# The first block of attention scores in three passes of split operands

## The chip, the cores and the metric

The kernel runs on one core of one Trainium2 chip. The metric is the device time of one execution in microseconds (us). The profile shows five engines of the core: TensorE for matrix products, with its weight loads shown apart, VectorE and ScalarE for element-wise work, GpSimd and SyncE, which here mostly issue transfers.

## What is computed

A decoder trunk of two layers over 256 tokens with width 1024, batch 1, all in float32. Layer 0 mixes tokens with a "forgetting" attention (a bias from cumulated log forget gates), layer 1 with a block-sparse attention whose block of 256 is here the whole sequence, so that it is causal attention with a relative-position bias. Each layer goes on with a SwiGLU feed-forward of width 2816 and a gated input embedding; a norm ends it. Both attentions have 16 heads of 64 and compute, for each head:

```python
logits = jnp.einsum('bhqd,bhkd->bhqk', qblk, k).astype(jnp.float32) * scale
logits = logits + cq[..., None] - c[:, :, None, :]          # layer 1: + table_ht[:, _t5_bucket(rel_o)]
logits = jnp.where(key_pos[None, :] <= t[:, None], logits, -jnp.inf)
probs = jax.nn.softmax(logits, axis=-1).astype(v.dtype)
return jnp.einsum('bhqk,bhkd->bhqd', probs, v)
```

Queries 0 to 127 see keys 0 to 127 alone; queries 128 to 255 see all 256.

## The kernel before

Most matmuls work on split operands. A float32 value x is kept as a high half, hi (x rounded to the type `float32r`), and a low half, lo = x - hi, and a product is three passes: hi·hi, hi·lo and lo·hi, each a matmul of `float32r`. `mm3` (lines 92 to 96) does so for the projections and the feed-forward. Weights arrive by DMA as float32; ScalarE copies them to the high half (line 169, 187 or 139) and VectorE subtracts for the low half (171, 188 or 142). TensorE loads the stationary operand of each matmul by an instruction of its own, which the profile shows as PEld.

An attention layer works on pairs of heads, j = 0 to 7; the two heads of a pair lie in partitions 0 to 63 and 64 to 127. For each pair `project(j, 0)` and `project(j, 1)` compute q and k, 24 matmuls of 128x128 by 256 columns each, into one bank `pq`. Then `project` scales the bank by the norm's rows into `t` ("qkt", line 563: q for 256 tokens, then k for 256), and makes the halves `th` ("qkh", 569, ScalarE) and `tl` ("qkl", 571, VectorE). These halves leave out the first 128 columns of `t`, the queries 0 to 127, so they hold 384 columns: q of the later 128 tokens and k of all 256.

`scores(*js)` (581) takes two pairs, four heads, at a time: after pairs 2, 4 and 6 for the two pairs before the last one projected, and once for pairs 6 and 7, with a part of the product for v between. So each layer has four calls. In a call each head has a bank `sp` with 384 columns: columns 0 to 127 are the first block (queries 0 to 127 against keys 0 to 127), columns 128 to 383 the other queries against all keys. In layer 0 four matmuls (405) first add the forget-gate bias to all 384 columns. Then the first block follows as a float32 matmul for each head, straight from `t` (589), and the other columns in three passes over the split halves (592), pass by pass, and the four heads in turn in each pass. In some calls the product of earlier pairs with v (674 and 676, float32) follows. VectorE then adds the mask or bias and takes minima (606), ScalarE exponentiates (610), and the results are transposed (644), sent through DMA to their place (651, 659) and read by `values`.

Each engine runs its instructions in the order in which they stand in its queue; the code places some by hand with `tc.issue_after`.

Of the kernel before, what the change touches and what calls it, by code (L numbers as in the profile page):

```python
# [28 lines left out]
F32R = mybir.dt.float32r  # L29
# [3 lines left out]
P = 128  # L33
S = 256
# [41 lines left out]
def trunk(ctx: ExitStack, tc: tile.TileContext, xg, wx, xr, pt, w, cst, gf, rel, hot, rvm, out):  # L76
    nc = tc.nc
    one = ctx.enter_context(tc.tile_pool(name="one", bufs=1))
    work = ctx.enter_context(tc.tile_pool(name="work", bufs=2))
# [4 lines left out]
    def bank(name):  # L84
        return ps.tile([P, 512], F32, tag="bank", name=name)

    def f32(ap):
        return ap.bitcast(F32)

    mm = nc.tensor.matmul  # L90

    def mm3(o, a, b, start, stop):
        (ah, al), (bh, bl) = a, b
        mm(o, ah, bh, start=start, stop=False, skip_group_check=True)  # L94
        mm(o, ah, bl, start=False, stop=False, skip_group_check=True)  # L95
        return mm(o, al, bh, start=False, stop=stop, skip_group_check=True)  # L96
# [353 lines left out]
    def enter(bks, x, w, k):  # L450

        steps = [(hf, a, 0, t) for hf in range(2) for a in range(2) for t in range(2)]
        if k == 0:
            steps[1:3] = steps[2:0:-1]
        for hf, a, b, t in steps + [(hf, 0, 1, t) for hf in range(2) for t in range(2)]:
            got = mm(bks[2 * t + hf], x[a][:, t * P:(t + 1) * P], w[b][:, hf * HC:(hf + 1) * HC],  # L456
                     start=k + a + b == 0, stop=k + b == KT, skip_group_check=True)
        return got

    def attention(layer, nm, mid, early, nf):  # L460
# [4 lines left out]
        def row(k, hf, w):  # L465
            for t in range(2):
                got = tokens(vb[2 * t + hf], nm.k(k), t, w, k == 0, k == KT - 1)
            return got

        def cut(wt, a):  # L470
            return [w[:, a * HC:(a + 1) * HC] for w in wt]

        for c in range(4):
            wt = [early.pop(0) if early else half() for _ in range(2 if c < 2 else 1)]
            for kk in range(2):
                k = 2 * c + kk
                if c > 1:
                    got = row(k, 0, cut(wt[0], kk))
                elif layer == 0:
                    got = enter(vb, nm.k(k), wt[kk], k)  # L480
                else:
                    for hf in range(2):
                        got = row(k, hf, cut(wt[kk], hf))
                if layer == 0 and k == KT - 2:
# [4 lines left out]
                    bias, add = rest()  # L489
# [25 lines left out]
        def second(c, wt):  # L515
            for kk in range(2):
                got = row(2 * c + kk, 1, cut(wt, kk))
            return got
# [20 lines left out]
        def weights(j, a):  # L539
            with held(j - 2), held("t" if j in BEHIND and a else None):  # L540
                if j in BEHIND and a == 0:
                    return gapped()
                return blocks(ENTRY if layer and j + a == 0 else ())

        def project(j, a):
            hi, lo = ahead.pop(0) if ahead else weights(j, a)
            if a == 0:
                pq[j] = bank(f"pq{layer}_{j}")
            bk = pq[j]
            for k in range(KT):  # L550
                mm3(bk[:, a * S:(a + 1) * S], (hi[k], lo[k]), nm.k(k),
                    start=(k == 0), stop=(k == KT - 1))
            if a == 0:
                return
            del pq[j]
            far = fresh[:]
            fresh.clear()
            if far:
                ahead.extend(weights(j + 1, i) for i in range(2 if j + 1 < NP else 0))
            for x in far[:1]:  # L560
                scaled(*x)
            t = work.tile([P, 2, S], F32, tag="qkt", bufs=3, name=f"qkt{layer}_{j}")
            got = nc.vector.tensor_tensor(t.rearrange("p a s -> p (a s)"), bk,
                                          nm.row.rearrange("p a s -> p (a s)"), op=ALU.mult)
            marks["t"] = marks.get(j - 1, (got,))[0], got
            th = work.tile([P, 3 * P], F32R, tag="qkh", bufs=3, name=f"qkh{layer}_{j}")
            tl = work.tile([P, 3 * P], F32R, tag="qkl", bufs=3, name=f"qkl{layer}_{j}")
            src = t.rearrange("p a s -> p (a s)")[:, P:]
            first = nc.scalar.activation(th, src, AF.Copy)
            with tc.issue_after(got.ins):  # L570
                got = nc.vector.tensor_tensor(tl, src, f32(th), op=ALU.subtract)
            marks[j] = first, got
            qk[j] = t, th, tl
            for x in far[1:]:
                with tc.issue_after(first.ins):
                    scaled(*x)
            with tc.issue_after(got.ins):
                for back in [turn(*x[:2]) for x in far]:
                    back()

        def scores(*js, then=None):

            rows = [slice(s * DH, (s + 1) * DH) for s in range(2)]
            heads = [(2 * j + s, d, qk[j], bank(f"sp{layer}_{2 * j + s}")) for j in js for s, d in enumerate(rows)]
            if add:
                for i, _, _, sp in heads:
                    add(i, sp)
            for _, d, (t, _, _), sp in heads:
                mm(sp[:, 0:P], t[d, 0, 0:P], t[d, 1, 0:P], start=add is None, stop=True, skip_group_check=True)
            for n, (q, k) in enumerate(((1, 1), (1, 2), (2, 1))):  # L590
                for _, d, t, sp in heads:
                    got = mm(sp[:, P:3 * P], t[q][d, 0:P], t[k][d, P:], start=False, stop=n == 2,
                             skip_group_check=True)
            if then is not None:
                with tc.issue_after(got.ins):
                    got = values(then)
            sl = (slice(0, P), slice(P, 3 * P))
            for n, j in enumerate(js):
                del qk[j]
                e = work.tile([P, 2, 3 * P], F32, tag="e", bufs=4, name=f"e{layer}_{j}")  # L600

                mn = tiny.tile([P, 2, 2, 2], F32, tag="mn", bufs=4, name=f"mn{layer}_{j}")
                for s in range(2):
                    i, _, _, sp = heads[2 * n + s]
                    for q, b in enumerate(bias(i)):
                        marks["low"] = nc.vector.tensor_tensor_reduce(e[:, s, sl[q]], sp[:, sl[q]], b, 1.0, 3.0e38,
                                                                      ALU.add, ALU.min, mn[:, 0, s, q:q + 1])
                for s in range(2):
                    for q in range(2):
                        last = nc.scalar.activation(e[:, s, sl[q]], e[:, s, sl[q]], AF.Exp, scale=-1.0,  # L610
                                                    bias=mn[:, 0, s, q:q + 1], accum_out=mn[:, 1, s, q:q + 1])
                marks["e", j] = last,
                fresh.append((j, e, mn))
            return got
# [9 lines left out]
        def scaled(j, e, mn):  # L624

            rc = inverse(j, mn)
            for s in range(2):
                for q, c in enumerate((slice(0, P), slice(P, 3 * P))):
                    nc.scalar.activation(e[:, s, c], e[:, s, c], AF.Copy, scale=rc[:, s, q:q + 1])
            return rc  # L630
# [36 lines left out]
        def values(j):  # L667

            po = bank(f"po{layer}_{j}")
            heads = [(slice(s * DH, (s + 1) * DH), slice((2 * i + s) * DH, (2 * i + s + 1) * DH), pts.pop(2 * i + s),  # L670
                      po[:, (i - j) * S:(i - j + 1) * S]) for i in (j, j + 1) for s in range(2)]
            for n in (0, 2):
                for d, c, t, o in heads[n:n + 2]:
                    mm(o[d], v[:, 0, c], t[:, 0:2], start=True, stop=False, skip_group_check=True)
                for d, c, t, o in heads[n:n + 2]:
                    got = mm(o[d, P:S], v[:, 1, c], t[:, 2], start=False, stop=True, skip_group_check=True)
            marks["o"] = split(oh[:, j:j + 2], ol[:, j:j + 2], po.rearrange("p (j s) -> p j s", s=S))
            return got

        for j in range(NP):  # L680
            project(j, 0)
            if layer and j == 0:
# [5 lines left out]
                bias, add = mid(nm)()  # L688
# [3 lines left out]
            if j + 1 in BEHIND:  # L692
                got = scores(j - 2, j - 1, then=0 if j == 6 else None)
# [26 lines left out]
        def split_late(after):  # L720
            with held(after):
                return half()

        got = second(2, split_late(6))
# [3 lines left out]
        with tc.issue_after(got.ins):  # L728
            got = scores(NP - 2, NP - 1, then=2)
# [8 lines left out]
        with tc.issue_after(got.ins):  # L738
            got = second(3, wt)
        keep(1)  # L740
        got = behind(got, "mid", 0)
        got = behind(got, "low", 1, 2)
        with tc.issue_after(got.ins):
            got = values(4)
        marks["third"] = marks["o"]
        got = behind(got, "seven", 3, 4)
        with tc.issue_after(got.ins):
            got = values(6)
# [245 lines left out]
    for layer in range(2):  # L994
# [5 lines left out]
        got = []  # L1000
# [127 lines left out]
```

## Time and profile before

| | us |
|---|---|
| median of 3 runs | 634.96 |
| lowest and highest run | 634.74, 635.93 |
| the profiled execution | 634.63 |
| its span, from the first to the last instruction | 632.8 |

The profile is one execution seen by the hardware profiler. Times of a line are in us, means of one instruction in ns. TensorE's matmuls are pipelined: a matmul's duration in the rows is the time from its start to its end, while the next one starts long before that end, so the time that it costs is read from the chain, or from starts. An operand of type `float32r` stands as f32 in the rows of matmuls. A float32 matmul appears as two records. TensorE's granted clock over the span was 0.997 of its upper level, 2.4 GHz.

### The profile page before, as it was taken

What the parts mean: (1) busy time and instruction counts of PE and PEld (TensorE: products, weight loads), DVE (VectorE), ACT (ScalarE), POOL (GpSimd) and SP (SyncE); (2) the same over time, 40 slices, a digit from 0 to 9 for tenths busy, and PEclk for the clock granted to TensorE, in tenths of its full rate; (3) what the DMA queues carried; (4) which work ended last, traced back from release to release, by engine and by line L of the source; (5) the groups of instructions that cost most, each with busy time, mean ns of one, the idle gap of its engine ahead of it and who ended that gap; (6) DMA issues with size and microseconds to landing.
All of it is one profiled execution on the core that took longest, in us unless ns stands there. A gap on an engine that the chain in (4) does not pass through costs nothing.

```text
span 632.8 us, 13104 instructions
## 1 busy us (share of the span) xinstructions
PE 624.2 (99%) x5241; PEld 602.8 (95%) x5241; DVE 467.7 (74%) x757; ACT 384.7 (61%) x663; POOL 43.4 (7%) x85
## 2 busy tenths in 40 slices
PE   9999999999999999999999999999999999999995
PEld 6899989999999999999989998999999999999984
DVE  6888888886666666668894898979666666666695
ACT  6668887754444445448774798768444444454653
POOL 0103340000000000000000044100000000000001
PEclk9999999999999999999999999999999999999998
DMA  8767878398766666666574698855766666665622
GB/s 336 259 192 236 252 241 314 120 351 259 244 206 197 199 193 208 193 208 180 191 239 171 205 295 232 296 197 180 256 199 186 195 197 202 200 208 180 197 50 85
DMA packets 41885, 135.27 MB, mean 214 GB/s; under 512 B 5248, under 2 KB 10848, under 8 KB 41824
## 3 DMA queue, kind: packets, MB, share of 16 engines
q1 hardware_dynamic: 37616, 124.11, 60.8%
q0 software_dynamic: 3488, 9.44, 5.1%
q10 hardware_dynamic: 720, 0.89, 0.4%
q8 instruction: 41, 0.67, 0.4%
q14 instruction: 20, 0.16, 0.1%
HBM read 126.01 MB, written 8.15 MB: 212 GB/s over the span
## 4 chain that ended last, share of the span: by engine, by line
PE 92%; DVE 3%; DMA 1%; issue 1%; SPq 1%; ACT 0%; POOL 0%; POOLq 0%; DVEq 0%; ACTq 0%
PE gu L95 13%; PE gu L94 13%; PE gu L96 13%; PE fo L96 6%; PE fo L95 6%; PE fo L94 6%; PE pq L94 5%; PE pq L96 5%; PE pq L95 4%; PE wo L94 2%; PE wo L95 2%; PE wo L96 2%; PE v L94 2%; PE v L95 2%; PE v L96 2%; PE v L456 1%
## 5 line engine op out<-in xcount | busy, mean ns | idle before, releaser
L171 DVE TENSOR_TENSOR wlo<-raw,whi 128x1024 fp32r<-128x1024 f32 (+1 forms) x168 | 203.5, 1216 | 65.1 <-ACT whi L169 64.8
L169 ACT ACTIVATE whi<-raw 128x1024 fp32r<-128x1024 f32 x166 | 173.7, 1056 | 94.4 <-issue 42.5
L95 PE MATMUL gu<-g,whi 128*128 128x256 f32 x704 | 194.7, 277 | 0.0
L94 PE MATMUL gu<-g,whi 128*128 128x256 f32 x704 | 194.6, 276 | 0.0
L96 PE MATMUL gu<-g,wlo 128*128 128x256 f32 x704 | 194.5, 276 | 0.0
L96 PEld LDWEIGHTS gu<-g,wlo 128*128 128x128 f32 x704 | 132.3, 188 | 0.0
L95 PEld LDWEIGHTS gu<-g,whi 128*128 128x128 f32 x704 | 132.2, 188 | 0.1
L94 PEld LDWEIGHTS gu<-g,whi 128*128 128x128 f32 x704 | 132.2, 188 | 0.0
L96 PE MATMUL fo<-fp,wlo 128*128 128x256 f32 x352 | 97.3, 276 | 0.0
L95 PE MATMUL fo<-fp,whi 128*128 128x256 f32 x352 | 97.2, 276 | 0.0
L94 PE MATMUL fo<-fp,whi 128*128 128x256 f32 x352 | 97.2, 276 | 0.0
L94 PE MATMUL pq<-g,whi 128*128 128x256 f32 x256 | 71.5, 279 | 0.0
L96 PE MATMUL pq<-g,wlo 128*128 128x256 f32 x256 | 70.9, 277 | 0.1
L95 PE MATMUL pq<-g,whi 128*128 128x256 f32 x256 | 70.8, 277 | 0.0
L188 DVE TENSOR_TENSOR wlo<-raw,whi 128x1080 fp32r<-128x1080 f32 x36 | 46.1, 1282 | 29.9 <-ACT whi L187 29.9
L94 PEld LDWEIGHTS fo<-fp,whi 128*128 128x128 f32 x352 | 66.1, 188 | 0.0
L95 PEld LDWEIGHTS fo<-fp,whi 128*128 128x128 f32 x352 | 66.1, 188 | 0.0
L96 PEld LDWEIGHTS fo<-fp,wlo 128*128 128x128 f32 x352 | 66.1, 188 | 0.0
L187 ACT ACTIVATE whi<-raw 128x1080 fp32r<-128x1080 f32 x36 | 39.6, 1101 | 28.6 <-PE gu L95 27.1
L94 PEld LDWEIGHTS pq<-g,whi 128*128 128x128 f32 x256 | 48.1, 188 | 1.0 <-issue 0.3
L96 PEld LDWEIGHTS pq<-g,wlo 128*128 128x128 f32 x256 | 48.2, 188 | 0.3 <-DVE wlo L171 0.3
L95 PEld LDWEIGHTS pq<-g,whi 128*128 128x128 f32 x256 | 48.1, 188 | 0.1
(194 smaller groups left out, 1038.8 us busy)
## 6 DMA issues: line engine op xcount, KB each, us to landing
raw<-w SPq DMA_DIRECT2D x177, 512.0 KB, 4.4
raw<-w SPq DMA_DIRECT2D x36, 540.0 KB, 4.3
dt<-turn POOLq DMA_DIRECT2D x10, 384.0 KB, 3.4
pt<-dt POOLq DMA_DIRECT2D x40, 96.0 KB, 5.2
d<-d SPq DMA_DIRECT2D x4, 768.0 KB, 7.1
bias<-d SPq DMA_DIRECT2D x4, 512.0 KB, 7.7
pt<-turn POOLq DMA_DIRECT2D x16, 96.0 KB, 3.1
pt<-turn SPq DMA_DIRECT2D x8, 96.0 KB, 3.3
```

Of the source, the lines that this page charges most:

```text
L94: mm(o, ah, bh, start=start, stop=False, skip_group_check=True)
L95: mm(o, ah, bl, start=False, stop=False, skip_group_check=True)
L96: return mm(o, al, bh, start=False, stop=stop, skip_group_check=True)
L169: state["hi"] = state[f"hi{i}"] = nc.scalar.activation(hi[:, c], raw[:, c], AF.Copy)
L171: nc.vector.tensor_tensor(lo[:, c], raw[:, c], f32(hi[:, c]), op=ALU.subtract)
L187: nc.scalar.activation(ht, raw[:, 0:WW], AF.Copy)
L188: state["lo"] = nc.vector.tensor_tensor(lt, raw[:, 0:WW], f32(ht), op=ALU.subtract)
L456: got = mm(bks[2 * t + hf], x[a][:, t * P:(t + 1) * P], w[b][:, hf * HC:(hf + 1) * HC], start=k + a + b == 0, stop=k + b == KT, skip_group ...
```

## The change

The halves `th` and `tl` are made of all 512 columns of `t`, so that they also hold the queries 0 to 127. The float32 matmul of the first block is gone; the three passes now go over two blocks, b = 0 (128 queries by 128 keys, 128 columns) and b = 1 (128 queries by 256 keys, 256 columns, as before). In each pass the four heads' matmuls of b = 0 come first, then those of b = 1. `t` is no longer read by TensorE. In layer 1, where no bias comes first, the first pass of b = 0 starts the bank.

```diff
-            th = work.tile([P, 3 * P], F32R, tag="qkh", bufs=3, name=f"qkh{layer}_{j}")
-            tl = work.tile([P, 3 * P], F32R, tag="qkl", bufs=3, name=f"qkl{layer}_{j}")
-            src = t.rearrange("p a s -> p (a s)")[:, P:]
+            th = work.tile([P, 4 * P], F32R, tag="qkh", bufs=3, name=f"qkh{layer}_{j}")
+            tl = work.tile([P, 4 * P], F32R, tag="qkl", bufs=3, name=f"qkl{layer}_{j}")
+            src = t.rearrange("p a s -> p (a s)")
             first = nc.scalar.activation(th, src, AF.Copy)
             with tc.issue_after(got.ins):
                 got = nc.vector.tensor_tensor(tl, src, f32(th), op=ALU.subtract)
...
-            for _, d, (t, _, _), sp in heads:
-                mm(sp[:, 0:P], t[d, 0, 0:P], t[d, 1, 0:P], start=add is None, stop=True, skip_group_check=True)
             for n, (q, k) in enumerate(((1, 1), (1, 2), (2, 1))):
-                for _, d, t, sp in heads:
-                    got = mm(sp[:, P:3 * P], t[q][d, 0:P], t[k][d, P:], start=False, stop=n == 2,
-                             skip_group_check=True)
+                for b in range(2):
+                    for _, d, t, sp in heads:
+                        got = mm(sp[:, b * P:(2 * b + 1) * P], t[q][d, b * P:(b + 1) * P], t[k][d, S:S + (b + 1) * P],
+                                 start=add is None and n == b == 0, stop=n == 2, skip_group_check=True)
```

## Rows read from the trace of the kernel before

**Rows 1.** The page's busy us of each engine, share of the span, instructions.
```profile
PE 624.2 (99%) x5241; PEld 602.8 (95%) x5241; DVE 467.7 (74%) x757; ACT 384.7 (61%) x663; POOL 43.4 (7%) x85
```

**Rows 2.** The page's chain that ended last, as shares of the span by engine.
```profile
PE 92%; DVE 3%; DMA 1%; issue 1%; SPq 1%; ACT 0%; POOL 0%; POOLq 0%; DVEq 0%; ACTq 0%
```

**Rows 3.** Waits of weight loads: engine, line, whom; us in total, times, longest.
```profile
PEld v L456 <- ACT g L207: 1.4, 2, 0.8
...
PEld pq L96 <- DVE wlo L171: 0.3, 1, 0.3
```

**Rows 4.** The chain in order of time, layer 0's second call: start us, us, what.
```profile
53.66 0.11 PE pq L95
53.77 0.11 PE pq L96
53.89 0.54 PE sp L405 x4
54.43 0.44 PE sp L589 x8
54.87 0.71 PE sp L592 x12
55.59 0.32 PE pq L94
```

**Rows 5.** The chain in order of time, layer 1's last call.
```profile
386.39 0.65 PE sp L589 x8
387.03 0.71 PE sp L592 x12
387.74 0.36 PE po L674
```

**Rows 6.** Instructions that write `sp`, the whole span: count, ns min/median/max, first and last start.
```profile
L589 PE MATMUL sp<-qkt x64: 267/272/373, 41.3 to 386.8; 64*128 64x128 f32 x64
...
L592 PE MATMUL sp<-qkh x32: 276/318/362, 41.7 to 387.0; 64*128 64x256 f32 x32
```

**Rows 7.** The chain in order of time, split operands with 512 columns.
```profile
75.99 0.23 PE v L96
76.22 0.23 PE v L94
```

**Rows 8.** Weight loads by shape: count, busy us, mean ns, idle before.
```profile
L676 PEld LDWEIGHTS po<-pt,v 128*64 128x64 f32 x64 | 4.6, 137 | 2.3
...
L592 PEld LDWEIGHTS sp<-qkh 64*128 64x128 f32 x32 | 2.5, 188 | 0.0
...
L377 PEld LDWEIGHTS pf<-hw,wg 128*32 128x32 f32 x14 | 0.4, 109 | 0.2
```

**Rows 9.** Timeline of weight loads and matmuls: start, us, what; short windows show two.
```profile
53.82 0.18 PEld L405 LDWEIGHTS sp<-c,sel 64*128 64x128 f32 x2
53.82 0.30 PEld L405 LDWEIGHTS sp<-c,sel 64*128 64x128 f32 x4
...
68.33 0.14 PEld L674 LDWEIGHTS po<-pt,v 128*64 128x64 f32 x2
68.33 0.20 PEld L674 LDWEIGHTS po<-pt,v 128*64 128x64 f32 x4
...
54.83 0.31 PEld L592 LDWEIGHTS sp<-qkl,qkh 64*128 64x128 f32 x4
54.95 0.40 PE L592 MATMUL sp<-qkl,qkh 64*128 64x256 f32 x4
```

**Rows 10.** The chain in order of time, float32 products with v.
```profile
69.20 0.43 PE po L674 x4
69.63 0.22 PE po L676 x4
```

**Rows 11.** ScalarE's copies to a high half by shape: busy us, mean ns.
```profile
L569 ACT ACTIVATE qkh<-qkt 128x384 fp32r<-128x384 f32 x16 | 8.3, 521 | 13.8 <-DVE qkt L563 13.7
...
L319 ACT ACTIVATE phi<-p 128x512 fp32r<-128x512 f32 x2 | 1.3, 634 | 0.1
```

**Rows 12.** VectorE's subtractions for a low half by shape.
```profile
L571 DVE TENSOR_TENSOR qkl<-qkt,qkh 128x384 fp32r<-128x384 f32 x16 | 8.9, 554 | 6.5 <-ACT qkh L569 6.4
...
L320 DVE TENSOR_TENSOR plo<-p,phi 128x512 fp32r<-128x512 f32 x2 | 1.4, 684 | 0.0
```

**Rows 13.** Timeline around layer 1's last call: ScalarE and VectorE.
```profile
384.40 0.53 ACT L569 ACTIVATE qkh<-qkt 128x384 fp32r<-128x384 f32 x1 [0.65 <-DVE qkt L563]
...
385.42 0.55 DVE L571 TENSOR_TENSOR qkl<-qkt,qkh 128x384 fp32r<-128x384 f32 x1
...
389.54 0.30 DVE L606 CUSTOM_DVE_ANT_0 e<-sp,bias 128x128 f32<-128x128 f32 x1
```

**Rows 14.** Timeline of VectorE where the first pairs are projected, both layers.
```profile
33.27 0.56 DVE L571 TENSOR_TENSOR qkl<-qkt,qkh 128x384 fp32r<-128x384 f32 x1
33.74 1.31 DVE L171 TENSOR_TENSOR wlo<-raw,whi 128x1024 fp32r<-128x1024 f32 x1
...
343.32 1.23 DVE L171 TENSOR_TENSOR wlo<-raw,whi 128x1024 fp32r<-128x1024 f32 x1 [0.39 <-ACT whi L169]
```

**Rows 15.** Timeline of the loads that read those low halves first.
```profile
35.22 0.19 PEld L96 LDWEIGHTS pq<-g,wlo 128*128 128x128 f32 x1
...
344.78 0.19 PEld L96 LDWEIGHTS pq<-g,wlo 128*128 128x128 f32 x1
```

## Prediction

> **What bounds the kernel now.** I read the busy table first [rows 1]: TensorE is busy in 624.2 of the 632.8 us, its weight loads in 602.8, VectorE in 467.7. The chain that ended last [rows 2] agrees: 92% of it lies on TensorE and 3% on VectorE. Then the waits of TensorE and of its weight loader [rows 3]: the largest is 1.4 us, before the attention begins, and only one, of 0.3 us, is for the low half of a weight tile while q and k are projected. So a microsecond of TensorE time added to a score stage should lengthen the run by that microsecond, as long as nothing else becomes late. The score stage itself I read in the chain in order of time, which gives each group of matmuls the time by which it moves the end. A call of `scores` in layer 0 takes 0.54 us for four bias matmuls, 0.44 for the first block, 0.71 for the other columns [rows 4]; in layer 1, where there is no bias matmul and the first block follows a full-width matmul, 0.65 and 0.71 [rows 5]. There are eight calls, four in each layer; in five of the other six the same groups take the same times to 0.01 us, and in the first one the chain mixes them with the bias table's matmul.
>
> The heads of a pair sit in the two row halves, and their matmuls run side by side: the rows of this stage come two at a time. So I count slots, one slot being two heads' matmuls. The first block has four heads and 64 records in 32 matmuls [rows 6], two records for each float32 matmul: 8 records, 4 slots in a call, 0.44 / 4 = 0.11 us each. The other columns are 12 records, 6 slots, 0.71 / 6 = 0.118 us each, with 256 columns.
>
> **The change, part by part.** *Removed:* 4 slots of float32 with 128 columns, 4 x 0.11 = 0.44 us a call. In layer 1 the 0.65 us are 0.44 and about 0.21 for the switch from full-width matmuls, which whatever comes first will pay.
>
> *Added:* three passes with 128 columns for four heads, 12 records, 6 slots a call. *Unchanged:* the 6 slots of 256 columns, 0.71 us. What a slot of split operands with 128 columns costs the trace doesn't show: no such matmul has under 256 columns. Bounds:
>
> From below, streaming alone. Split operands take 0.23 us for 512 columns and 0.11 to 0.12 for 256 [rows 4, 7], so 128 columns would take 0.059, half of a slot of 0.118. Six slots are then 0.35, and a call gains 0.09.
>
> Between, the weight load. Each matmul brings its own 128 weight columns. The time of a load grows with its columns: 109 ns for 32, 137 for 64, 188 for 128 [rows 8]; from 64 to 128 that is 51 ns for 64 columns, 0.8 ns a column. How close loads can follow each other shows where TensorE drains before the bias matmuls: there two pairs of loads start together with nothing streaming between them. One pair takes 0.18 us, both 0.30, so the second starts 0.11 to 0.12 us after the first; with 64 weight columns the figures are 0.14 and 0.20, so 0.06 [rows 9]. A load of 128 columns occupies its path for about 0.11 us, and it runs beside the matmul before it. A matmul of 256 columns just covers it; one of 128 columns in 0.059 us can't. The slot is then 0.11, the load's: six are 0.66.
>
> From above, that the operand type doesn't help at 128 columns and each pass costs what a float32 matmul costs, two records of 0.11: 0.22 a slot, 1.32 a call.
>
> I take 0.11, the load's. It is worked out from loads of the same shape (64x128) in the same stage, while the bound below assumes loads that the trace shows nowhere and the bound above needs a fallback for which no row speaks. That the old slots of 128 float32 columns also take 0.11 proves nothing either way: float32 passes with only 64 weight columns scale with the moving columns, 0.43 us for two slots of 256 and 0.22 for two of 128 [rows 10], so they are bound by their own streaming at half speed. The change removes four slots bound by streaming and puts six bound by loading in their place.
>
> Sum: (6 - 4) x 0.11 = 0.22 us a call, 8 calls: +1.76 us. If the new slots take 0.118 like those of 256 columns, it is (0.71 - 0.44) x 8 = +2.2.
>
> The Trainium skill speaks against this price. Its page "TensorE: Matmul & The Clock Gate", section "Back-to-back issue gap", gives a sustained spacing of about 81 ns for load and matmul pairs with N = 128; by that, an estimate, a call would be 6 x 0.081 - 0.44 = +0.05 and the run +0.4 us. The trace here doesn't agree for 128 weight columns of four bytes: its spacing of loads is 0.11.
>
> *Splitting.* The copy to the high half and the subtraction for the low half grow from 384 to 512 columns, 16 times each. Rows of 512 columns exist: ScalarE 634 against 521 ns, +113 ns; VectorE 684 against 554, +130 ns [rows 11, 12]. Over the kernel that is 1.8 us of ScalarE and 2.1 of VectorE. I cost them at nothing but one spot. Their readers: scores of two pairs come after the project of the third, so most halves are ready whole microseconds early. The tightest is the last pair of layer 1. Its VectorE subtraction starts at 385.42 and takes 0.55, so it ends at 385.97, while the first matmul of its scores starts at about 386.39 [rows 5, 13]. Both extensions together, 0.24 us, leave 0.18; and the low half is first read in the second pass, four slots later. The new order makes the first block wait for the high half where it waited for the product alone, but that half is there at 384.93.
>
> Queued behind the subtraction on VectorE are the low halves of weight tiles. The closest is at the start of layer 0: the subtraction of pair 0 runs at 33.27, the weight subtraction at 33.74 for 1.31 us, to 35.05, and the load that reads it starts at 35.22 [rows 14, 15]. So 0.17 us are there for 0.13, and a semaphore's delay of some 0.06 takes part of it: I put down 0.05 us. At the same place of layer 1 the weight subtraction waits for ScalarE, whose copy is 0.11 longer: it takes 1.23 us from 343.32, to 344.55, and its load is at 344.78 [rows 14, 15]. That is 0.23 us for 0.11 and the semaphore. If the cover were gone at each of the 16 places, it would cost up to 16 x 0.13 = 2.1 us.
>
> *Behind the scores.* Their readers on VectorE start late by themselves: the last call of layer 1 ends at about 387.74 and its first minimum runs at 389.54 [rows 5, 13], VectorE being busy in between. The 0.22 us shift the matmuls that read the results by as much as the scores. The larger tiles (3 KB more a partition) and 32 more records on TensorE (24 for 20 in each call) cost nothing that I see. No DMA, no wait on POOL or SP is moved.
>
> Total: +1.8 us. The profiled execution took 634.63 us, 632.8 of it the span; so 636.4 for its like. The median of the runs is 634.96, 0.33 above it; the forecast against the median is 636.7.
>
> **The rivals.** *Streaming decides* (the loads are hidden, 0.059 to 0.081 a slot): (0.35 - 0.44) x 8 = -0.7 us up to +0.4, so 634.3 to 635.3, not slower. It decides if the load of one slot can start before the matmul of the slot before it, so that loads run ahead during the 256-column slots. Against it: the loads of a pass begin 0.12 us before its matmuls (54.83 and 54.95), one slot and no more [rows 9].
>
> *The new operands don't give their speed at 128 columns*, so that the change doesn't do what it says: each of the 96 new matmuls costs a float32 matmul, 0.22 a slot. 6 x 0.22 - 0.44 = +0.88 a call, +7.0 us, 642.0. For it: everywhere in this kernel matmuls of split operands have 256 columns or more, and those of 128 are float32, so no row excludes it. Against it: at 256, 384 and 512 columns they cost the same per column.
>
> *The cover is gone*: VectorE is busy in almost the whole of each score stage, and 16 subtractions are longer. With +1.8 from TensorE and up to 2.1 from VectorE that is up to 638.9. Against it: the waits show one of 0.3 us in all of this stretch, and TensorE itself gets later by 0.22 a call, which gives VectorE back more than the 2 x 0.13 that it loses.
>
> **How the numbers follow.** Forecast (slots bound by the load) 0.60, 636.2 to 637.4; streaming 0.11; float32 price 0.20; cover gone 0.09. The range leaves out the float32 price alone: from 634.3 to 638.8. A change of 0.2% is 1.27 us, about what a measurement of this kernel can tell from none. The forecast's +1.8 is beyond it; I give 0.08 of its 0.60 to a result that falls short of +1.27 since slots are somewhat cheaper or the runs scatter by 0.5. Slower: 0.52 + 0.20 + 0.07 = 0.79; same: 0.08 + 0.09 + 0.02 = 0.19; faster by over 0.2%: 0.02, what of streaming lies beyond -1.27.
>
> **What would show it.** In the profile after, the chain should have one group of 24 score records of about 1.37 us a call in layer 0 (1.15 before) and 1.58 in layer 1 (1.36). Pairs of 128 columns should start 0.11 us apart, with 96 records in all: 0.06 is the streaming case, 0.22 or 192 records the float32 case. The stage's weight loads should stand back to back. The copies should take about 0.63 us and the subtractions 0.68, with no new wait of TensorE for a low half except some hundredths at 35 us. The forecast is wrong if TensorE waits for halves of q and k, or if the sum of the eight groups grows by 1.8 us and the span doesn't.

## The result, and the profile after

The changed kernel takes 639.63 us (median of 6 runs, 639.44 to 640.51) where the kernel before, in runs beside it, takes 634.83: a ratio of 1.0077, 95% interval 1.0064 to 1.0090, or +4.8 us. The forecast was +1.8, the range ended at 638.8. The direction was right, the size wrong by a factor of 2.7.

The page of the changed kernel, its busy times and the chain's shares, answers [rows 1, 2]:

```profile
span 638.7 us, 13180 instructions
...
PE 628.4 (98%) x5273; PEld 606.3 (95%) x5273; DVE 469.1 (73%) x757; ACT 386.2 (60%) x663; POOL 43.5 (7%) x85
...
PE 85%; DVE 6%; ACT 3%; issue 2%; DMA 2%; POOL 1%; SPq 0%; POOLq 0%; DVEq 0%; ACTq 0%
```

TensorE's busy time grew by 4.2, but the span by 5.9, so TensorE stands idle for 1.7 us more. (The profiled execution took 640.51 us, 0.9 over the median, 634.63 before; so the trace's lags add up to more than 4.8.) The larger news is the chain: TensorE's share fell from 92 to 85%, and VectorE, ScalarE and transfers took it. A chain that leaves the bounding engine says that this engine now waits somewhere.

The score group of the chain, third call of layer 1 (the form of [rows 5]; start us, us, what):

```profile
377.67 1.58 PE sp L591 x24
```

That is 0.22 over the 0.65 + 0.71 of before, as forecast. The slots alone can't explain the result. The waits of TensorE and of its weight loader do (engine, line, whom; us in total, times, longest), beside [rows 3]:

```profile
PE po L673 <- DMA pt<-dt: 1.4, 1, 1.4
...
PE pq L94 <- DVE qkt L563: 0.4, 1, 0.4
PE sp L591 <- ACT qkh L569: 0.2, 1, 0.2
...
PEld sp L591 <- ACT qkh L569: 0.6, 2, 0.3
...
PEld sp L591 <- DVE qkl L571: 0.4, 2, 0.2
```

None of these was there before. To see where they cost, I laid the two traces side by side by the start of the same matmul behind each score group; the table is the growth of the lag there, in us. The third column is the first experiment below, the changed kernel with the order of instructions put back.

| Growth of the lag behind | changed kernel | changed, old order |
|---|---|---|
| layer 0, calls 1 to 3 | 0.20, 0.25, 0.22 | 0.19, 0.25, 0.22 |
| the product with v behind call 3 | 0.11 | 0 |
| layer 0, call 4 | 0.71 | 0.23 |
| layer 1, calls 1 to 3 | 0.26, 0.30, 0.23 | 0.26, 0.30, 0.23 |
| the product behind call 3 | 0.51 | 0 |
| layer 1, call 4 | 0.91 | 0.22 |
| inside the product behind call 4 | 1.60 | 0 |
| projections of layer 1, matmuls further apart | some 0.4 | some 0.3 |

Six calls pay the forecast's 0.2 or little more: read from the matmul just ahead of a group to the one just behind it, each of the six takes 0.21 to 0.23 in the changed kernel, and each of all eight in the third column. What the table has above that in layer 1 belongs, with its last row, to the matmuls between calls 1 and 2. They start 0.118 us apart where the kernel before has 0.113, as the starts of a matmul and of the ninth behind it show (kernel before, then changed kernel in the old order):

```profile
355.76 0.28 PE L94 MATMUL pq<-g,whi 128*128 128x256 f32 x1
...
356.78 0.28 PE L94 MATMUL pq<-g,whi 128*128 128x256 f32 x1
```
```profile
356.75 0.28 PE L96 MATMUL pq<-g,wlo 128*128 128x256 f32 x1
...
357.81 0.28 PE L96 MATMUL pq<-g,wlo 128*128 128x256 f32 x1
```

Over the 96 matmuls there that is 0.4 us; its cause stays open. The rest of the changed kernel's lag sits at the last two calls of each layer.

Why there? VectorE is late, and the timeline of the first call in layer 0 shows how. VectorE in the kernel before (start us, us, engine, line, op), with ScalarE's first exponential:

```profile
43.63 1.21 DVE L171 TENSOR_TENSOR wlo<-raw,whi 128x1024 fp32r<-128x1024 f32 x1
44.76 0.27 DVE L606 CUSTOM_DVE_ANT_0 e<-sp,con 128x128 f32<-128x128 f32 x1
...
45.08 0.41 ACT L610 ACTIVATE e<-e,mn 128x128 f32<-128x128 f32 x1 [0.97 <-DVE mn L606]
```

The same stretch of the changed kernel:

```profile
43.84 2.34 DVE L171 TENSOR_TENSOR wlo<-raw,whi 128x1024 fp32r<-128x1024 f32 x2
46.11 0.27 DVE L605 CUSTOM_DVE_ANT_0 e<-sp,con 128x128 f32<-128x128 f32 x1
...
46.42 0.40 ACT L609 ACTIVATE e<-e,mn 128x128 f32<-128x128 f32 x1 [2.13 <-DVE mn L605]
```

Two weight subtractions stand ahead of the minima where one stood. No line of the diff asks for that. The order of instructions that the code doesn't place by hand is made by the planner when the program is built, and a listing of both programs shows that it moved them: seven low halves of weight tiles went from behind the minima to ahead of them (one in each of layer 0's calls 1 and 2, two in each of layer 1's, one in its call 3), and three splits of a product with v went a few instructions back. Nothing else differs in the order on VectorE, ScalarE, GpSimd and SyncE.

In this first call the moved subtraction makes the minima about 1.1 us later than the scores alone would; the exponentials start later; and the reciprocals, which VectorE reaches sooner with its subtraction already done, stand and wait for them. The waits of VectorE, kernel before and then changed kernel:

```profile
DVE rc L621 <- ACT e L610: 3.5, 7, 1.3
```
```profile
DVE rc L620 <- ACT e L609: 9.2, 8, 1.6
```

VectorE lost 5.7 us in these waits. The delay is handed from call to call within a layer. The first minimum of layer 1's third call, kernel before and then changed kernel:

```profile
377.43 0.29 DVE L606 CUSTOM_DVE_ANT_0 e<-sp,bias 128x128 f32<-128x128 f32 x1
```
```profile
383.77 0.28 DVE L605 CUSTOM_DVE_ANT_0 e<-sp,bias 128x128 f32<-128x128 f32 x1
```

It starts 6.3 us later, while the scores that it reads are 2.7 later, so 3.6 are VectorE's own. By the same reading VectorE's own delay is 1.1, 2.2, 2.2 and 1.0 us in the four calls of layer 0, and 2.2, 3.3, 3.6 and 0.7 in those of layer 1; in the changed kernel with the old order it is at most 0.1 anywhere. So TensorE pays only at the last two calls of a layer, when the delay has grown. At the end of layer 1 the lag meets TensorE (changed kernel, timeline of VectorE, ScalarE and TensorE):

```profile
388.30 0.18 DVE L620 RECIPROCAL rc<-mn 128x4 f32<-128x4 f32 x1 [1.06 <-ACT e L609]
388.39 0.66 DVE L563 TENSOR_TENSOR qkt<-pq,row 128x512 f32<-128x512 f32 x1
...
389.56 0.61 ACT L569 ACTIVATE qkh<-qkt 128x512 fp32r<-128x512 f32 x1
...
390.23 0.33 PE L591 MATMUL sp<-qkh 64*128 64x128 f32 x2 [0.20 <-ACT qkh L569]
...
394.25 0.44 PE L673 MATMUL po<-pt,v 128*64 128x256 f32 x2 [1.43 <-DMA pt<-dt]
```

In the kernel before the scaling of q and k for this pair waited for TensorE, the right way round:

```profile
383.68 0.69 DVE L563 TENSOR_TENSOR qkt<-pq,row 128x512 f32<-128x512 f32 x1 [1.10 <-PE pq L96]
```

Now it comes directly behind the reciprocal, the high half is ready at 390.17 (384.93 by [rows 13]), TensorE has been waiting, and behind the scores it waits again for transposed results that come through DMA.

### The profile page after: what moved, and what is told of

It reads as the page before. It is cut to its first block, busy times and chain, and to the rows that moved or that the text cites. A ratio compares the mean times of both kernels' runs of the same rounds, so it can differ in the third digit from the quotient of the medians.

```text
span 638.7 us, 13180 instructions
## 1 busy us (share of the span) xinstructions
PE 628.4 (98%) x5273; PEld 606.3 (95%) x5273; DVE 469.1 (73%) x757; ACT 386.2 (60%) x663; POOL 43.5 (7%) x85
## 4 chain that ended last, share of the span: by engine, by line
PE 85%; DVE 6%; ACT 3%; issue 2%; DMA 2%; POOL 1%; SPq 0%; POOLq 0%; DVEq 0%; ACTq 0%
PE gu L95 13%; PE gu L96 13%; PE gu L94 13%; PE fo L96 6%; PE fo L94 6%; PE fo L95 6%; PE pq L96 3%; PE pq L94 3%; PE pq L95 3%; PE wo L94 2%; DVE wlo L171 2%; PE wo L96 2%; PE wo L95 2%; PE v L456 2%; ACT e L609 2%
```

## The experiments

**The old order back.** Is the order the cause, or the longer copies, or the new passes? This kernel has all of the change, and edges (`tc.issue_after`, which puts an instruction behind another) that hold the order of the kernel before on VectorE and ScalarE (its order is that of before on every engine but TensorE).

```diff
+        def late(j, a):
+            return tc.issue_after(marks["low"].ins) if j in (4, 6) and (layer or a) else nullcontext()
...
-                return blocks(ENTRY if layer and j + a == 0 else ())
+                with late(j, a):
+                    return blocks(ENTRY if layer and j + a == 0 else ())
...
+                      with tc.issue_after(marks["o"][1].ins) if n + s == 2 and then == 2 * layer else nullcontext():
...
+                      with tc.issue_after(marks["o"][0].ins) if n + s > 0 and (then == 0 or layer and then == 2) else nullcontext():
...
-            with held(after):
+            with held(after), tc.issue_after(marks["low"].ins) if layer and after == 6 else nullcontext():
                 return half()
```

> The changed kernel with one thing put back: VectorE and ScalarE run their instructions in the order of the kernel before (seven low halves of weight tiles behind the minima of a score call instead of ahead of them, the split of three products with v back between the minima and exponentials). Nothing is left out; TensorE runs the changed kernel's matmuls. Theory 1 (TensorE's two more slots a call cost 8 x 0.22 = 1.8 us, the rest of the 4.8 us is the moved order): 636.6 us, between 636.3 and 637.1, ratio to the kernel before 1.0028, no wait of TensorE for a high half at the fourth calls. Rival (the longer copies and subtractions, or the new order of the passes, make VectorE late by themselves): still over 638.5 us with those waits.

Measured: 636.35 us against 634.29 of before beside it, ratio 1.0032 (1.0020 to 1.0045). Its chain's shares, then the chain in its second call of layer 0 and its last of layer 1, then all that TensorE waited for:

```profile
PE 93%; DVE 4%; issue 1%; DMA 0%; ACT 0%; SPq 0%; POOL 0%; POOLq 0%; DVEq 0%; ACTq 0%
```
```profile
53.92 0.54 PE sp L405 x4
54.46 1.38 PE sp L595 x19
...
388.20 1.58 PE sp L595 x24
```
```profile
PE cold L114 <- PEq L1125: 0.8, 1, 0.8
```

(Where a group has under 24 records, some are missing from the trace.) The chain is TensorE's again, the waits are gone, and the third column of the table has 0.2 to 0.3 at every call and beyond that only its last row. So +2.0 us is the price of the changed kernel without the new order, nearly all of it the matmuls', and some 2.8 of the 4.8 came with the order.

**Only the weight subtractions back.** The same without the two edges on the split of the product with v; against the kernel above:

```diff
-                      with tc.issue_after(marks["o"][1].ins) if n + s == 2 and then == 2 * layer else nullcontext():
...
-                      with tc.issue_after(marks["o"][0].ins) if n + s > 0 and (then == 0 or layer and then == 2) else nullcontext():
```

> The changed kernel with the seven low halves of weight tiles put back behind the minima, while the split of the products with v stays where the changed kernel has it. Theory 1 (the weight subtractions ahead of the minima are what costs): 636.6 us, as with the whole order put back, within 0.3 us. Rival (the split of the product with v, which comes later and releases its bank later, is the cost): about 638 us or more.

Measured: 636.52 us, ratio 1.0036 (1.0022 to 1.0050). The seven weight subtractions are the cost; the later splits add nothing that shows.

**The moved order in the kernel before.** The other way round: matmuls and halves of before, but the minima and exponentials of calls 1 and 2 are recorded after the next weight tiles and held behind the last of them. It moves six of the seven. With them, in three of the calls, the scaling of the next pair's q and k goes ahead of the second reciprocal, so the order isn't the changed kernel's in every place.

```diff
+            for rest_of in put:
+                with tc.issue_after(state["lows"].ins):
+                    rest_of()
...
+            def minima():
...
+            if then is None:
+                pending.append(minima)
+            else:
+                minima()
```

> The kernel before with its own matmuls and halves, but the low halves of weight tiles in the first and second call of each layer (six of the seven) ahead of the minima, as in the changed kernel. Theory 1 (order and TensorE's slots add up): 637 us, +1.5 to +3 over the kernel before, with waits of TensorE at the fourth call of a layer. Rival (the order costs only together with longer halves): 634.8 us, within 0.3 of the kernel before.

Measured: 637.13 us, ratio 1.0046 (1.0033 to 1.0058), about +2.9. TensorE's waits are of the same kind, in other places (its page of waits):

```profile
PE wo L95 <- DVE o L320: 0.8, 1, 0.8
...
PE pq L94 <- DVE qkt L568: 0.5, 2, 0.3
PE po L684 <- DMA pt<-dt: 0.3, 1, 0.3
```

I had expected them at the fourth calls; by their starts the waits for `qkt` and for the transposed results fall behind the third calls (69.36 in layer 0, 378.65 and 379.86 in layer 1), and the output projection's wait of layer 0 (104.80) for the low half of `o` was not foreseen. VectorE's own delay of the minima grows as in the changed kernel, to 2.3 us in layer 0 and 3.7 in layer 1. The size is: +2.9 from the order alone, +2.0 from the change alone, +4.8 from both. That they add up so closely is in part luck, since this kernel moves six and not seven and pays in other places; that the order costs this much without the change's matmuls is shown.

**Longer halves alone.** Halves of 512 columns, the first block still float32; against the kernel before:

```diff
-            th = work.tile([P, 3 * P], F32R, tag="qkh", bufs=3, name=f"qkh{layer}_{j}")
-            tl = work.tile([P, 3 * P], F32R, tag="qkl", bufs=3, name=f"qkl{layer}_{j}")
-            src = t.rearrange("p a s -> p (a s)")[:, P:]
+            th = work.tile([P, 4 * P], F32R, tag="qkh", bufs=3, name=f"qkh{layer}_{j}")
+            tl = work.tile([P, 4 * P], F32R, tag="qkl", bufs=3, name=f"qkl{layer}_{j}")
+            src = t.rearrange("p a s -> p (a s)")
...
-                    got = mm(sp[:, P:3 * P], t[q][d, 0:P], t[k][d, P:], start=False, stop=n == 2,
+                    got = mm(sp[:, P:3 * P], t[q][d, P:2 * P], t[k][d, 2 * P:], start=False, stop=n == 2,
```

> The kernel before with high and low halves of all 512 columns, and the first block still in float32: the copies and subtractions are longer, TensorE's work is the same. One weight subtraction of layer 0's first call goes behind the minima instead of ahead of them. Theory 1 (the longer halves are hidden): 634.8 us, within 0.3 of the kernel before. Rival (VectorE is the bound in the score stages): up to 2.1 us more, 636.9.

Measured: 634.51 us, ratio 0.9999 (0.9991 to 1.0008). The longer copies and subtractions are hidden. The one weight subtraction that goes behind the minima here doesn't pay for them: side by side, the lag against the kernel before is the same 0.15 us ahead of the first score call and behind the last.

**One layer's order back.** Only layer 0 gets the old order, by the edges of the first experiment with one more condition each.

```diff
-            return tc.issue_after(marks["low"].ins) if j in (4, 6) and (layer or a) else nullcontext()
+            return tc.issue_after(marks["low"].ins) if not layer and j in (4, 6) and (layer or a) else nullcontext()
...
```

> The changed kernel with the old order on VectorE and ScalarE in layer 0 alone; layer 1 keeps the changed kernel's. Theory 1 (each layer pays for its own moved instructions, where TensorE waits at the end of its scores; by matmuls laid side by side the changed kernel loses 0.6 us more than the slots in layer 0 and some 2.3 in layer 1): about 0.6 below the changed kernel, so 638.5 us or +4.2 over the kernel before. Rival (layer 0's moves delay everything behind them): 637 us or less.

Measured: 638.55 us against 634.24, ratio 1.0063 (1.0051 to 1.0076), +4.0 by the ratio and +4.3 by the medians, where the whole change gave +4.8. So layer 0's moves cost under 1 us; against the 636.35 of the old order in both layers, layer 1's cost 2.2. What TensorE waits for lies in layer 1 alone:

```profile
PE po L679 <- DMA pt<-dt: 0.8, 2, 0.6
...
PE sp L595 <- ACT qkh L573: 0.4, 1, 0.4
```

VectorE's delay isn't handed on from layer to layer: in layer 1 its own delay of the minima is 2.2, 3.3, 3.6 and 0.7 us, as in the changed kernel, though layer 0 now has none.

**The price of a new slot: passes.** All that follow have the old order but for an instruction or two (here one weight subtraction of layer 0's first call goes behind the minima). This one leaves out the second and third pass of the first block.

```diff
+                    if n and not b:
+                        continue
```

> The changed kernel in the old order on VectorE and ScalarE, with the first block's second and third pass left out (hi by lo and lo by hi are not added for queries 0 to 127), so 4 of the 6 new slots of a call are gone. One weight subtraction of layer 0's first call goes behind the minima. Theory 1 (a new slot costs 0.11 us, the weight load): 32 slots less, 3.5 us below the run with three passes in the old order, so 632.8 us, 1.5 below the kernel before. Streaming price (0.059 a slot): 1.9 below, 634.4 us. Float32 price (0.22): 7 below, 629.3.

Measured: 633.57 us, ratio 0.9986 (0.9977 to 0.9995). The score groups shrank as the 0.11 says, 4 x 0.11 = 0.45 a call (second of layer 0, second of layer 1):

```profile
54.21 0.93 PE sp L597 x16
...
362.00 1.13 PE sp L597 x16
```

That is 3.6 us over eight calls, but the time fell by about 2.9: TensorE, which is now earlier, waits at layer 1's output projection (side by side, 0.6 us of the gain are lost there; the weight loader's wait for `o`, line 320, is 0.5).

**The price of a new slot: columns.** Second and third pass over 64 instead of 128 columns, with the same weight loads.

```diff
+                    w0 = DH if n and not b else (b + 1) * P
...
-                        got = mm(sp[:, b * P:(2 * b + 1) * P], t[q][d, b * P:(b + 1) * P], t[k][d, S:S + (b + 1) * P],
+                        got = mm(sp[:, b * P:b * P + w0], t[q][d, b * P:(b + 1) * P], t[k][d, S:S + w0],
```

> The changed kernel in the old order, with the second and third pass of the first block over 64 columns instead of 128 (the keys 64 to 127 get the first pass alone there), all weight loads as they were. Theory 1 (the load of 128 weight columns sets the slot): no change, 636.3 us as with 128 columns, pairs of 64 columns start 0.11 us apart. Rival (those matmuls stream at half speed, 128 columns in 0.11 us): 32 slots by 0.055 less, 1.8 below, 634.5 us, and starts 0.055 apart.

Measured: 636.44 us, ratio 1.0033 (1.0023 to 1.0042): no change. Timeline of the loads of two passes in layer 1, with 128 columns (changed kernel) and then with 64, and the latter's group in the chain:

```profile
365.36 0.53 PEld L591 LDWEIGHTS sp<-qkl,qkh 64*128 64x128 f32 x8
365.82 0.53 PEld L591 LDWEIGHTS sp<-qkh,qkl 64*128 64x128 f32 x8
```
```profile
364.89 0.53 PEld L596 LDWEIGHTS sp<-qkl,qkh 64*128 64x128 f32 x8
365.35 0.53 PEld L596 LDWEIGHTS sp<-qkh,qkl 64*128 64x128 f32 x8
```
```profile
364.51 1.57 PE sp L596 x24
```

In both, a pass of two short and two long slots takes 0.46 us from its first load to the next pass's; 0.24 of it are the long ones (0.118 each), so 0.11 is left for a short one, with 128 columns or with 64. Half the columns are worth nothing. Nor is it a fixed price of each matmul: a slot can start 0.03 behind the last (below), but over a pass the slots come no faster than the loads. My expectation put the proof in the matmuls' starts, 0.11 apart; in the rows the starts in a pass are uneven (the second pair of 64 columns follows the first by 0.03, the next by 0.11), and it is the loads that come evenly, 0.11 to 0.12 apart.

**Slots in turn.** Slots of 128 and 256 columns alternate.

```diff
-                for b in range(2):
-                    for _, d, t, sp in heads:
...
+                for x in range(0, len(heads), 2):
+                    for b in range(2):
+                        for _, d, t, sp in heads[x:x + 2]:
...
```

> The changed kernel in the old order, with the slots of 128 and 256 columns in turn (a pair's two heads with 128, then the same two with 256) instead of two and two. Theory 1 (a load can run only during the slot ahead of its own): no change, 636.3 us. Rival (loads can run further ahead, and use the slots of 256 columns): up to 48 x 0.05 = 2.4 below, 633.9 us.

Measured: 636.65 us, ratio 1.0032 (1.0019 to 1.0044), the same 1.58 us a call in layer 1 (its last call in the chain):

```profile
388.17 1.58 PE sp L596 x24
```

So a load gains nothing from a longer slot further ahead.

**What makes the planner move them** was looked at in listings of built programs alone, not on the chip. With longer halves and no new pass, or with one new pass, none of the seven is ahead of the minima (one of layer 0's goes the other way). With two passes, or with three of which two have 64 columns, four are ahead; with three full passes, seven. So it goes by the matmuls in front of the minima, and not by their number alone: three passes move seven or four, by their columns, which on the chip cost nothing here. That it places by an estimate of when the scores are done is my reading of this; it wasn't tried.

## Why the prediction was wrong, point by point

*What bounds the kernel:* right for the kernel before, and for the changed one in the old order (93% of the chain on TensorE).

*A slot of 0.11 us, bound by the load of 128 weight columns:* right as far as tested; no run varied the weight columns themselves. The groups of the chain grew by 0.22 to 0.24 us, the passes by their number and not by their columns. The streaming rival and the float32 rival are both out; the 96 matmuls have one record each and 0.11 us a slot. The Trainium skill's spacing of 81 ns ("TensorE: Matmul & The Clock Gate", section "Back-to-back issue gap") doesn't hold for these weights: over a pass, no run here has slots of split operands under 0.11.

*The sum of the slots:* +1.76 against +2.0 measured in the old order, whose interval, 1.3 to 2.9 us, holds both. Read directly at the eight groups the trace gives 1.8. The matmuls 0.118 apart in layer 1 add some 0.4, whose cause I didn't find, and a start 0.2 earlier in this execution takes half of it back; that the sum comes so near is in part luck.

*Splitting costs nothing but 0.05:* right within 0.6 us, by the kernel with longer halves alone (634.51 against 634.29); a term of 0.05 is too small to see. The copies measured 628 ns and the subtractions 692, as put down.

*Behind the scores:* here the prediction failed. It costed VectorE with the queue of the kernel before: "Their readers on VectorE start late by themselves", and a weight subtraction only ever delayed by 0.13 us by what is longer ahead of it. It never asked whether the queue stays the same. The planner put seven weight subtractions, 8.5 us of VectorE, ahead of minima that a chain of exponentials, reciprocals, transposes and transfers hangs on. That is 2.8 of the 3.0 us between the forecast's +1.8 and the result's +4.8, shown in both directions: put back, they vanish; six of them moved in the kernel before, +2.9 appear. The prediction's own sign of being wrong, that TensorE waits for halves of q and k, came true (0.2 us, and 1.0 of its weight loader), but for the order and not for the longer halves.

*The rival "cover gone"* looks like what happened, and reached 638.9, but for another reason: it priced 16 longer subtractions, which cost nothing. What the profile of before did show is how tight that chain is: VectorE busy in nearly all of each score stage, which the prediction names for this rival alone, and ScalarE's exponentials directly behind the minima. Where it says that VectorE is "busy in between" ahead of the minimum at 389.54, the work just ahead of it is weight subtractions:

```profile
388.38 1.27 DVE L142 TENSOR_TENSOR wlo<-raw,whi 128x256 fp32r<-128x256 f32 x2
```

A price for one more of them there, 1.2 us of VectorE's lag in a call, could have been read from the rows.

No version here that keeps all three passes beats the kernel before; the one with a single pass is 0.9 us below it by the ratio (633.57 against 634.24) and leaves out two of the three products of halves. The float32 block takes 4 slots of 0.11; three passes take 6 of at least the same.

## What to carry to other kernels

Where the order of instructions is made by a planner, a change to one engine's work can reorder another's: list both programs engine by engine before looking for the time anywhere else, and hold the order that matters by edges. In a stream of matmuls with 128 columns of four-byte weights, count weight loads and not columns: here a slot costs 0.11 us over 64 columns and 0.118 over 256. And work that has slack (next weights) queued ahead of a chain that has none (minima, exponentials, transposes) can cost time though nothing was added: here VectorE later waited 5.7 us more for what it had delayed, and the kernel took 2.8 us more.

## What the runs showed of the hardware

Matmuls of split operands over 64, 128 and 256 columns take 0.11 to 0.12 us a slot alike; I had expected 64 to tell the two theories apart, but not so exactly (1.57 against 1.58 us a call). Matmuls of one shape, 128x128 by 256 columns, stand 0.113 us apart in most stretches and 0.118 in some, whatever the kernel; no run here shows what decides it. And when TensorE is made 3.6 us faster in the score stages, 0.6 of it is lost in a wait at layer 1's output projection: there VectorE has little slack on the other side too.
